# Moving the lag table, the output stage's loads and the stores inside the front of an encoder layer

## The chip, the cores and the metric

The kernel runs on one core of a Trainium2 chip. The metric is the device time of one execution in microseconds (us); lower is better. The profile names the engines PE (TensorE matmul), PEld (its weight load), DVE (VectorE), ACT (ScalarE), POOL (GpSimd) and SP (SyncE). Each engine works through its own instructions in order; SP's and POOL's also issue DMAs.

## The reference, cut to what matters

```python
h = layer_norm(x, ln_in_g, ln_in_b)                       # x: 1024 rows of 1024
proj = jnp.einsum('bld,de->ble', h, w_in)                 # 2048 columns
rq, rk, rv, rg, su, aq, ak, av = jnp.split(proj, ...)
y_ret = retention(rq, rk, rv, rg, ret_theta)              # 4 heads, chunks of 128, states forward and backward
y_ssm = s5_mixer(su, ...)                                 # 16 groups of 16 channels, 64 complex states, both ways
y_att = window_sink_attention(aq, ak, av, attn_sink)      # 8 query heads, 2 key heads, window 128
mix = concat(y_ret, y_ssm, y_att) @ w_out
h = layer_norm(ALPHA * h + mix, ln1_g, ln1_b)
ffn = expert_choice_ffn(h, router_w, w_gate, w_up, w_down)   # 16 experts, each takes its best 128 rows
h = layer_norm(ALPHA * h + ffn, ln2_g, ln2_b)

def s5_mixer(u, ...):
    lam_bar = exp(lam * step);  bu = b_bar @ u            # per group, forward and reversed
    states = associative_scan(a, b -> a2*a1, a2*b1 + b2)  # complex, along the 1024 rows
    y = gelu(real(c @ states) + d * u)
    return y * sigmoid(y @ w_glu + b_glu)
```

## The kernel before

The program has three parts. The *front* makes the input norm, all projections, the retention head group and the S5 mixer. The *attention part* makes the windowed attention, the output projection, the second norm and the router. The *expert part* streams 384 MB of expert weights and ends with the last norm. Float32 products of the projections are made of three matmuls on halves (`split` into high and low, `mm3`, lines 74 to 76).

The order inside the front is written out by hand. `front` puts functions at places on a line of numbers (`at(place, fn)`, `spread`), `Plan.run` calls them sorted by place, and every engine keeps that order. So a place sets the order on each engine and in each DMA queue; it is no time. A function that is placed early but waits holds up all that is behind it on its engines. After the front a scheduler merges the attention part's instructions with the end of the front, without changing the front's own order.

The S5 mixer works in blocks of 8 rows, so the scan runs over 128 positions. `Params` makes the powers of the decay; `outputs` and `outputs_store` make the output weights `wo_d`, which go to DRAM; `jumps` makes the powers over 8 to 128 rows (`LT`, `A`). `s5_input` stores the projected input in `ut_d`, `s5_input_load` reads it back turned as `U`, and `u_d` keeps it. `s5_states_part` multiplies it into `VS`, which holds 2 x 16 x 128 values on each partition. `s5_scan` runs 15 steps inside 8 blocks of 16 positions, then 7 steps from block to block; `s5_carry` adds the carry; `s5_states_store` writes the states `s_d`. `Lags` makes the products inside a block (the table `KC`, stored as `m_d`), and `Output` sums `m_d` times the input and `wo_d` times the states, with gelu and gate, into `YO` and `y_d`. `Matrix` loads and splits the output projection's weights.

Memory sets much of the order. Pools are opened and closed inside the front: `VS` lies where `Params` lay, so it can only be written when all of that pool has been stored. The pool `raw` has two buffers named `wraw` of 8 KB per partition, through which all weights pass. `K.ast` has three buffers under the tag `k4` (the split keys, values and queries `kst`) and three under `q2`.

The projections after the first are units named in `order`: `K0`, `K1`, `V0`, `V1` and `q00` to `q31` are products of 24 matmuls with 512 columns, `g0` to `g7` are retention gates, `r0` to `r7` retention chunks, and `l` a gap. `V0` in the code is also the place of the first unit.

## Time and profile before

| | |
|---|---|
| median of 3 runs | 1772.43 us (1767.63 to 1777.95) |
| profiled execution | 1771.64 us |
| its span from first to last instruction | 1769.9 us |
| busy: PE, DVE, ACT | 92%, 80%, 64% of the span |
| mean granted clock of PE | 0.962 |

The front ends about 392 us after the span's start, the attention part about 640 us, and the rest belongs to the experts. In the profile's lines "L643" is line 643 of the kernel, `out<-in` are the program's names, and a wait is idle time of an engine with what ended it. PEclk is the clock that was granted to PE, as a share of full speed.

### The profile page before, as it was taken

To read this page: it belongs to the slowest core of one execution; us is meant where nothing else is said; L and a number is where in the kernel's file an instruction comes from. 1 tells how busy PE (TensorE), PEld (TensorE's weight loads), DVE (VectorE), ACT (ScalarE), POOL (GpSimd) and SP (SyncE) were. 2 spreads that over 40 slices of the span, in tenths; PEclk is the share of its full clock that TensorE was granted. 3 is DMA by queue.
4 is the path that set the end of the run, shared out by engine and by line. 5 is a ranking of instruction groups with operands and counts; after the bars stand their busy time and mean duration, and the time that the engine had idled before them with its cause. 6 is when DMAs were issued, how large, how long until landed. Compare 5 with 4: busy or idle time off the path is not lost.

```text
span 1769.9 us, 21221 instructions
## 1 busy us (share of the span) xinstructions
PE 1628.6 (92%) x7760; PEld 1315.0 (74%) x7760; DVE 1415.4 (80%) x1748; ACT 1124.1 (64%) x1259; POOL 194.5 (11%) x214
## 2 busy tenths in 40 slices
PE   6987886479999989999999999999999999999996
PEld 4866775357777767888888888888888777777785
DVE  7856863154666899899888898898898989999995
ACT  4615232275555467777777777777777787777773
POOL 1000010100100101010110100100101232231221
PEclk9999988678999989999999999999999999999998
DMA  5452336853321489999999999999999999999993
GB/s 210 162 139 79 86 98 167 248 206 104 102 66 72 154 337 363 378 399 392 376 365 397 368 366 392 368 383 389 358 388 393 385 399 388 393 401 387 404 402 142
DMA packets 110713, 513.61 MB, mean 290 GB/s; under 512 B 12048, under 2 KB 35856, under 8 KB 59792
## 3 DMA queue, kind: packets, MB, share of 16 engines
q1 hardware_dynamic: 100480, 482.36, 71.9%
q0 software_dynamic: 10128, 29.89, 5.5%
q8 instruction: 61, 1.00, 0.2%
q14 instruction: 44, 0.36, 0.1%
HBM read 465.02 MB, written 47.19 MB: 289 GB/s over the span
## 4 chain that ended last, share of the span: by engine, by line
PE 58%; DVE 14%; DMA 12%; issue 8%; ACT 7%; SPq 2%; POOL 0%; POOLq 0%; DVEq 0%; ACTq 0%
PE gu L1699 24%; PE y L1699 12%; DVE whl L1746 6%; PE mm L74 4%; DMA wraw<-in_exp_w_down 4%; PE mm L75 4%; PE mm L76 4%; DMA zz<-acc_d 4%; ACT whl L1739 2%; PE tp L1684 1%; PE tp L1249 1%; ACT S L1229 1%; PE sm L1343 1%; DMA wraw<-in_exp_w_up 1%; SPq L754 1%
## 5 line engine op out<-in xcount | busy, mean ns | idle before, releaser
L1746 DVE TENSOR_TENSOR whl<-wraw,whl 128x2048 fp32r<-128x2048 f32 x384 | 873.3, 2288 | 97.9 <-ACT whl L1739 97.1
L1739 ACT ACTIVATE whl<-wraw 128x2048 fp32r<-128x2048 f32 x384 | 734.6, 1917 | 243.7 <-PE gu L1699 79.7
L1699 PE MATMUL gu<-whl,xT 128*128 128x512 f32 x3072 | 740.0, 397 | 0.0
L1699 PEld LDWEIGHTS gu<-whl,xT 128*128 128x128 f32 x3072 | 570.4, 189 | 125.1
L1699 PE MATMUL y<-whl,hT 128*128 128x512 f32 x1536 | 368.6, 395 | 0.7 <-ACT hT L65 0.7
L1699 PEld LDWEIGHTS y<-whl,hT 128*128 128x128 f32 x1536 | 288.3, 188 | 69.8 <-ACT hT L65 0.9
L1673 POOL DMA_INDIRECT xs<-h_d,index x15 | 41.3, 2756 | 741.1 <-PE y L1699 553.1
L74 PE MATMUL mm<-hT,whl 128*128 128x512 f32 x160 | 68.6, 429 | 0.5 <-ACT gate L352 0.5
L75 PE MATMUL mm<-hT,whl 128*128 128x512 f32 x160 | 65.1, 407 | 0.0
L76 PE MATMUL mm<-hT,whl 128*128 128x512 f32 x160 | 64.8, 405 | 0.0
L65 ACT ACTIVATE hT<-tp 128x512 fp32r<-128x512 f32 x80 | 45.9, 583 | 27.9 <-PE tp L1684 15.8
L66 DVE TENSOR_TENSOR hT<-tp,hT 128x512 fp32r<-128x512 f32 x80 | 54.1, 684 | 9.1 <-ACT hT L65 9.1
L74 PE MATMUL mm<-WO,yh 128*128 128x512 f32 x128 | 52.1, 407 | 4.2 <-ACT yh L65 4.0
L1684 PE MATMUL tp<-ident,hid 128*128 128x128 f32 x256 | 39.7, 279 | 14.9 <-DVE hid L1781 14.8
L1684 PEld LDWEIGHTS tp<-ident,hid 128*128 128x128 f32 x256 | 31.4, 142 | 27.0 <-DVE hid L1781 19.9
L75 PE MATMUL mm<-WO,yh 128*128 128x512 f32 x128 | 51.2, 400 | 0.0
L76 PE MATMUL mm<-WO,yl 128*128 128x512 f32 x128 | 50.4, 400 | 0.0
L1229 ACT ACTIVATE S<-S,asm 128x384 f32<-128x384 f32 (+1 forms) x64 | 36.9, 579 | 19.9 <-DVE asm L1225 19.9
L74 PE MATMUL mm<-whl,hT 128*128 128x512 f32 (+1 forms) x128 | 47.5, 371 | 1.2 <-ACT gate L352 1.2
L1222 DVE CUSTOM_DVE_ANT_0 S<-at,R,sink 128x384 f32<-128x384 f32 (+1 forms) x64 | 35.4, 579 | 15.5 <-PE at L1220 14.1
L75 PE MATMUL mm<-whl,hT 128*128 128x512 f32 (+1 forms) x128 | 45.8, 357 | 1.4 <-DVE whl L130 1.4
L76 PE MATMUL mm<-whl,hT 128*128 128x512 f32 (+1 forms) x128 | 45.3, 354 | 0.0
(426 smaller groups left out, 1837.0 us busy)
## 6 DMA issues: line engine op xcount, KB each, us to landing
wraw<-in_exp_w_gate SPq DMA_DIRECT2D x128, 1024.0 KB, 8.0
wraw<-in_exp_w_up SPq DMA_DIRECT2D x128, 1024.0 KB, 8.0
wraw<-in_exp_w_down SPq DMA_DIRECT2D x128, 1024.0 KB, 8.0
wraw<-in_w_in SPq DMA_DIRECT2D x8, 1024.0 KB, 6.0
x<-in_x SPq DMA_DIRECT2D x8, 512.0 KB, 4.5
h_d<-x SPq DMA_DIRECT2D x8, 512.0 KB, 3.1
q_d<-kst SPq DMA_DIRECT2D x32, 128.0 KB, 3.1
qs<-q_d POOLq DMA_DIRECT2D x16, 256.0 KB, 4.2
```

Of the source, the lines that this page charges most:

```text
L65: nc.scalar.activation(hi, src, AF.Copy)
L66: eng.tensor_tensor(lo, src, hi.bitcast(F32), OP.subtract)
L74: nc.tensor.matmul(ps, a[0], b[0], start=start, stop=False)
L75: nc.tensor.matmul(ps, a[0], b[1], start=False, stop=False)
L76: nc.tensor.matmul(ps, a[1], b[0], start=False, stop=stop)
L1222: nc.vector.tensor_tensor_reduce(s[:, :W], ps[:, :W], K.R[:, ro:ro + W], 2.0 ** -(h + 1), K.sink[:, h:h + 1], OP.add, OP.max, accum_out=m[ ...
L1229: nc.scalar.activation(S[g][:, :W], S[g][:, :W], AF.Exp, bias=nm[:, g:g + 1], accum_out=rs[:, g:g + 1])
L1673: nc.gpsimd.indirect_dma_start(out=xs, out_offset=None, in_=K.h1_dram, in_offset=bass.IndirectOffsetOnAxis(ap=K.index[:, e:e + 1], axis=0))
L1684: K.nc.tensor.transpose(pt[:, c, :], src[:, (c0 + c) * P:(c0 + c + 1) * P], K.ident)
L1699: nc.tensor.matmul(ps, a[s][c], u[:, t, i * w:(i + 1) * w], start=first and id(ps) not in began, stop=last and left[id(ps)] == 0)
L1739: self.K.nc.scalar.activation(u[:, 0, :], self.raw[k1].rearrange("p a b -> p (a b)"), AF.Copy)
L1746: self.K.nc.vector.tensor_tensor(u[:, 1, :], raw, u[:, 0, :].bitcast(F32), OP.subtract)
```

## The change

The change writes the front in another order and changes some instructions.

- The input norm's gain and shift are no longer broadcast by two DMAs of 512 KB. `Rows` loads two rows of 4 KB, and four matmuls with a selecting matrix spread them; ACT copies the products.
- The retention's constants, tables and states are placed earlier; half of the state steps go between the first projections.
- `outputs` and its stores stand ahead of the jumps, and the second pair of stores stands ahead of the store of `U` in SP's queue. `work` has two buffers and a third one, `wtmp`, holds the second product.
- `VS` is laid out by step: position in the block, then channel and block. A scan step reads and writes contiguous runs. The carry works on 8 channels at once (8 pairs of 840 elements for 16 pairs of 420). All states go to DRAM through ACT copies `SO` of 1024 elements.
- `Lags` is made in quarters right after the states' products, while the scan starts. It takes its buffers from `k4`, `q2` and `wraw`.
- `Output` loads its table, input and weights (`MUW`) into `wraw` buffers during the last projections. Its products are units `o0` to `o3` of the order. Weights come in rows of 128 elements out of 144.
- The turns of the retention chunks, their queries and scores, and the loads of `W6`, `W7` and the output projection's weights have other places.

```diff
-    for i in range(1, NT - 1):
-        for a in range(2):
+    for a in range(2):
+        for i in range(1, NT - 1):
...
-    return ops
+    return ops[0:NT - 2], ops[NT - 2:]
...
-        t = [self.pool.tile(sh, F32, name="work", bufs=3) for _ in range(2)]
+        t = [self.pool.tile(sh, F32, name=n, bufs=b) for n, b in (("work", 2), ("wtmp", 1))]
...
-        prev, cur = V5[:, :, :, :, r - 1], V5[:, :, :, :, r]
+        prev, cur = K.VS[:, :, r - 1], K.VS[:, :, r]
...
+def s5_states_store(K, d, ri):
...
+    SO = K.ast.tile([P, 8, P], F32, name="SO", tag="k4", bufs=3)
+    src = K.VS[:, ri, :, d * 8:d * 8 + 8, :].rearrange("p r q b -> p q b r")
+    dst = SO if d == 0 else SO[:, :, ::-1]
+    nc.scalar.activation(dst.rearrange("p q (b r) -> p q b r", r=16), src, AF.Copy)
+    for g2 in range(2):
+        nc.sync.dma_start(K.s_dram[d][g2][ri * 64:(ri + 1) * 64], SO[g2 * 64:(g2 + 1) * 64])
...
-    def load(self, g2, d):
+    def load(self, g2, d, q):
+        w = K.ast.tile([P, 4, 9, 16], F32, name="WO", tag="k4", bufs=3)
...
+        bx = K.ast.tile([P, 4, 16], F32, name="BX", tag="q2", bufs=3)
...
-            self.kc = self.pool.tile([16, 8, 15, 16], F32, name="KC")
+            self.kc = K.raw.tile([P, 8, 15, 16], F32, name="KC", tag="wraw")[0:16]
...
     def load(self, g2, q):
...
+        x = K.raw.tile([P, 4, 4, P], F32, name="MUW", tag="wraw")
+        nc.sync.dma_start(x[:, 0], K.m_dram[g2][:, gs])
+        nc.sync.dma_start(x[:, 1], K.u_dram[:, q * 8 + g2:q * 8 + 8:2, :])
+        for d in range(2):
+            n0 = 16 * (1 - d)
+            nc.sync.dma_start(x[:, 2 + d], K.wo_dram[d][g2][:, gs, n0:n0 + P])
...
+    def states(self, g2, q):
...
+            nc.sync.dma_start(z[:, :, 1 - d:P + 1 - d], K.s_dram[d][g2][:, q * 4:q * 4 + 4])
...
+class Rows:
...
+        self.x = pool.tile([P, D], F32, name="x", bufs=3)
+        for i, k in enumerate(("ln_in_g", "ln_in_b")):
+            K.nc.sync.dma_start(self.x[i:i + 1, :], I[k].rearrange("(a d) -> a d", a=1))
...
+    def select(self):
+        self.K.nc.vector.tensor_copy(self.sel, self.K.ident[0:2, 0:2, None].to_broadcast([2, 2, P]))
...
+    def spread(self, i, n):
+        K, ns = self.K, slice(n * 512, (n + 1) * 512)
+        ps = (K.pmm if i == 0 else K.pat).tile([P, 512], F32, name="mm" if i == 0 else "at")
+        K.nc.tensor.matmul(ps, self.sel[:, i, :], self.x[0:2, ns], start=True, stop=True)
+        K.nc.scalar.activation((K.g0, K.b0)[i][:, ns], ps, AF.Copy)
...
-    e = spread(B + 16.5, 0.15, par.jumps())
+    E0 = B + 26.0
+    e = B + 18.5
...
-    at(E0 + 1.0, lambda: s5_input_load(K))
-    at(E0 + 2.0, lambda: nc.sync.dma_start(K.u_dram, K.U))
+    at(E0 + 4.7, lambda: s5_input_load(K))
+    at(E0 + 5.2, WA.load)
+    at(E0 + 9.1, WG.load)
+    at(E0 + 14.0, lambda: nc.sync.dma_start(K.u_dram, K.U))
...
+    lp = [V0 - 4.0 + 1.6 * i + (1.0 if i > 3 else 0) for i in range(8)]
...
-    order = "K0 g0 g1 K1 r0 V0 r1 g2 g3 V1 r2 q00 r3 g4 g5 q01 r4 q10 r5 g6 g7 r6 q11 r7 q20 q21 l q30 l q31".split()
+    order = "K0 g0 g1 K1 r0 V0 r1 g2 g3 V1 r2 q00 r3 g4 g5 q10 r4 q01 r5 g6 g7 r6 q11 r7 q20 q30 q21 o0 o1 q31 o2 o3".split()
...
-            at(s + 8, c.turn)
+            at(s + 11, c.turn)
...
-    for k, (wt, prev) in enumerate(((W6, ("K1", "V1")), (W7, ("q01", "q11")))):
-        at(where[prev[0]] - 8, wt.load)
+    for wt, place, prev in ((W6, V0 + 15, ("K1", "V1")), (W7, where["r5"], ("q01", "q11"))):
+        at(place, wt.load)
...
+        at(max(e2 + 5.0, O + 0.2) + 0.1 * i if i < 2 else where[f"o{i - 2}"] + 3.1, lambda k=k: out.states(*k))
...
-        at(M0 + 0.1 if i < 2 else M0 + 4.6 + (i - 2) * 2.6, lambda i=i: X["mat"].load(2 * i))
+        at(where[f"o{i + 2}"] + 3.1 if i < 2 else G + 3.5 + (i - 1) * 2.5, lambda i=i: X["mat"].load(2 * i))
```

**Three places where the order changes.** First, SP's queue between the input projection of S5 and the keys. `ut_d` is the store of the projected input, `U` its turned load, `u_d` the store of that, and `wo_d` the output weights' stores. Before:

```order
L628 DMA ut_d<-uT 128x1024
L636 DMA U<-ut_d 16x16x128 x8
L1026 DMA u_d<-U 128x2048
L616 DMA wo_d_86<-work 64x1152
L616 DMA wo_d_87<-work 64x1152
L616 DMA wo_d_88<-work 64x1152
L616 DMA wo_d_89<-work 64x1152
```

The same stretch of SP's queue after:

```order
L633 DMA ut_d<-uT 128x1024
L621 DMA wo_d_86<-work 64x1152
L621 DMA wo_d_87<-work 64x1152
L641 DMA U<-ut_d 16x16x128 x8
L621 DMA wo_d_88<-work 64x1152
L621 DMA wo_d_89<-work 64x1152
L121 DMA wraw<-in_w_in 128x2048
```

The store of `U`, which waits until `U` has landed, stood ahead of three of the four pairs of output weights, and now stands behind all of them.

Second, SP's queue at the end of the projections, where the output stage's operands are loaded. `m_d` is the lag table, `q_d` the queries' store, `Z` the states. Before:

```order
L870 DMA q_d_1_76<-kst 256x1x128 x4
L754 DMA m_d_95<-KC 128x1x128 x8
L778 DMA M<-m_d_94 128x512
L780 DMA U<-u_d 128x4x128
L783 DMA WO_2862<-wo_d_86 128x576
L786 DMA Z_2864<-s_d_90 128x4x128
```

The place where `Z` is loaded after:

```order
L420 DMA y_d_71<-roT 128x256
L872 DMA q_d_1_76<-kst 256x1x128 x8
L420 DMA y_d_72<-roT 128x256
L764 DMA wg<-in_ssm_w_glu 128x512
L766 DMA bg<-in_ssm_b_glu 128x2
L790 DMA Z_2815<-s_d_90 128x4x128
L790 DMA Z_2818<-s_d_92 128x4x128
L790 DMA Z_2821<-s_d_90 128x4x128
L790 DMA Z_2824<-s_d_92 128x4x128
```

The lag table's stores are gone from here, the table, the input and the weights are loaded further ahead, and only the states still wait here, behind eight stores of queries.

Third, ACT at the end of the front. `KC` is the lag table, `kst` the last queries, `WO` with four digits the split of the output projection's weights, `YG` the gelu, `yT` its turned copy, `glu` the gate, and L1229 (after: L1255) the attention's exponentials. Before:

```order
L742 ACTIVATE KC<-at 16x4x128 x2
L744 ACTIVATE KC<-at 16x4x112 x2
L68 ACTIVATE kst<-mm,qscale 128x512
L65 ACTIVATE WO_2912<-wraw 128x1024 x2
L803 ACT_TABLE_LOAD
L803 ACTIVATE YG<-mm 128x4x8x16
```

ACT at the same end after:

```order
L68 ACTIVATE kst<-mm,qscale 128x512
L805 ACTIVATE YG<-mm 128x4x8x16 x2
L814 ACTIVATE yT<-tp 128x512 x4
L65 ACTIVATE WO_2992<-wraw 128x1024 x2
L827 ACTIVATE glu<-mm,hb 128x512
L1255 ACT_TABLE_LOAD
L1255 ACTIVATE S,asm<-S,asm 128x256
```

The lag table has left this place, and the four gelus stand together ahead of the weights' split, where they stood between its parts.

More of the change, by code (lines that the diff above doesn't have):

```diff
@@ L606, in outputs @@
         cr, ci = (self.C[:, i, q, None, :].to_broadcast(sh) for i in range(2))
-        t = [self.pool.tile(sh, F32, name="work", bufs=3) for _ in range(2)]
+        t = [self.pool.tile(sh, F32, name=n, bufs=b) for n, b in (("work", 2), ("wtmp", 1))]
         ve.tensor_tensor(t[0], cr, pr if ri == 0 else ni, OP.mult)
@@ L923, in front @@
     par = Params(K, I, X["s5a"])
-    norm[2].load()
-    spread(3.5, 0.01, ops[0:10])
+    at(6.0, norm[2].load)
+    at(2.9, rows.select)
+    for i in range(2):
+        for n in range(2):
+            at(3.3, lambda i=i, n=n: rows.spread(i, n))
+    spread(3.5, 0.01, ops[0:6])
     at(4.0, norm[0].stats)
-    spread(4.5, 0.01, ops[10:])
-    at(5.0, decays)
     at(7.0, norm[0].gain)
@@ L981, in front @@
         at(place, fn)
+    ahead, behind = retention_state(K)
+    for i, fn in enumerate(ahead):
+        at(S0 + T * (i + 3) + 2.55, fn)
     B = S0 + T * NT
@@ L1052, in front @@
     SC = E0 + 23.8
[L1053 to L1054 removed]
+    e = spread(SC, 3.7, steps)
+    e = spread(e, 1.6, blocks)
     fixes = s5_carry(K)
[L1056 to L1062 removed]
+    e2 = spread(e, 3.8, fixes)
+    for i in range(4):
+        at(e + (i + 1) * 7.6 + 0.05, lambda i=i: s5_states_store(K, i // 2, i % 2))
+    at(e2 + 1.0, lambda: close(X["s5v"][0]))
+    lag = lambda: X["lags"]
+    quarters = [(g2, d, q) for g2 in range(2) for d in (1, 0) for q in range(2)]
+    lp = [V0 - 4.0 + 1.6 * i + (1.0 if i > 3 else 0) for i in range(8)]
+    for i, (k, s) in enumerate(zip(quarters, lp)):
+        at(E0 + 18.0 + i * 0.1 if i < 3 else lp[i - 3] + 0.5, lambda k=k: lag().load(*k))
+        at(s, lambda k=k: lag().part(*k))
+        at(s + 1.0, lambda k=k: lag().put(*k))
+        if k[1:] == (0, 1):
+            at(s + 1.4, lambda k=k: lag().store(k[0]))
     ops, exps = retention_tables(K)
[L1066 to L1068 removed]
+    spread(E0 + 2, 0.3, ops)
+    at(E0 + 8.5, exps)
+    spread(E0 + 9.5, 1.0, behind)
     at(V0 - 0.9, lambda: X.update(retB=pool("retB", side="right")))
@@ L1075, in front @@
     where = {}
+    X["out"] = Output(K, I)
+    out = X["out"]
+    qs = [(g2, q) for g2 in range(2) for q in range(2)]
     for w in order:
@@ L1125, in front @@
             at(where[prev[i]] + 6.0, lambda wt=wt, i=i: wt.low(i))
-    R = where["r7"] + 12.5
-    def lags_space():
-        close(X["retB"][0], K.c_ret)
-        X["s5k"] = pool("s5k", side="right")
-        X["lags"] = Lags(K, I, X["s5k"][1])
-    at(R, lags_space)
-    lag = lambda: X["lags"]
-    quarters = [(g2, d, q) for g2 in range(2) for d in (1, 0) for q in range(2)]
-    at(R + 0.1, lambda: (lag().load(0, 1), lag().load(0, 0)))
-    lp = [R + 5 + 1.5 * i for i in range(8)]
-    for i, (k, s) in enumerate(zip(quarters, lp)):
-        at(s, lambda k=k: lag().part(*k))
-        at(s + 1.0, lambda k=k: lag().put(*k))
-        if i in (1, 3):
-            at(s + 1.1, lambda d=k[1]: lag().load(1, d))
-        if k[1:] == (0, 1):
-            at(s + 1.2, lambda k=k: lag().store(k[0]))
@@ L1144, in front @@
-    Z = R + 5 + 8 * 1.5 + 1.3
+    R = where["r7"] + 2.9 + 12.5
+    at(R, lambda: close(X["retB"][0], K.c_ret))
+    O = max(R, e2 + 1.0) + 0.1
     def output_space():
         X["s5o"] = pool("s5o")
-        X["out"] = Output(K, I, X["s5o"][1])
-    at(max(R + 3, e2 + 2.1), output_space)
-    out = lambda: X["out"]
-    qs = [(g2, q) for g2 in range(2) for q in range(2)]
-    end = where["q31"] + 5.6
-    O0 = max(Z + 5, end - 2.0)
+        out.space(X["s5o"][1])
+        out.bias()
+    at(O, output_space)
@@ L1154, in front @@
     for i, k in enumerate(qs):
[L1155 to L1158 removed]
+        at(where["q11"] + 8.5 + i * 0.1 if i < 2 else where[f"o{i - 2}"] + 3.0, lambda k=k: out.load(*k))
+        at(max(e2 + 5.0, O + 0.2) + 0.1 * i if i < 2 else where[f"o{i - 2}"] + 3.1, lambda k=k: out.states(*k))
@@ L1159, in front @@
+    G = s + 1.0
     mq = [(m, q) for q in range(2) for m in range(2)]
     for i, k in enumerate(mq):
-        at(G + i * 0.6, lambda k=k: out().turn(*k))
-        at(G + 2.6 + i * 2.0, lambda k=k: out().gate(*k))
-        at(G + 4.6 + i * 2.0, lambda k=k: out().gated(*k))
-    at(G + 12.0, lambda: (out().store(0), out().store(1)))
+        at(G + i * 0.6, lambda k=k: out.turn(*k))
+        at(G + 2.6 + i * 2.0, lambda k=k: out.gate(*k))
+        at(G + 4.6 + i * 2.0, lambda k=k: out.gated(*k))
```

188 lines of the change are left out of this document (81 added, 107 removed).

## Prediction

> **What bounds the kernel now.** PE carries most of the work, so what can be won lies where it waits. After the page I cut the span where the program changes its work and asked for each engine's busy time in each stretch (the view of windows):
>
> ```profile
> 121.00:157.60 36.60, 20.69 (x107) 18.47 (x108) 9.32 (x24) 12.45 (x20) 0.74 (x8) 0.81 0.46 101
> 157.60:281.90 124.30, 110.60 (x654) 94.80 (x653) 98.41 (x271) 46.75 (x105) 9.71 (x9) 0.93 0.36 99
> 281.90:321.60 39.70, 24.75 (x113) 17.16 (x112) 3.23 (x10) 6.67 (x13) 1.33 (x6) 0.79 0.58 153
> 321.60:392.20 70.60, 40.80 (x172) 30.90 (x173) 25.80 (x63) 35.08 (x67) 6.92 (x15) 0.71 0.78 252
> 392.20:650.00 257.80, 236.50 (x1205) 187.10 (x1203) 180.77 (x498) 147.00 (x306) 22.43 (x66) 0.95 0.37 131
> ```
>
> The columns are PE, PEld, DVE, ACT and POOL busy, then PE's granted clock. The front ends at 392.2 with the last `YO`. Inside it three stretches are poor: 121.0 to 157.6, and above all 281.9 to 392.2, where nobody is busy even half of the time but PE, and PE runs at a clock of 0.7 to 0.8. The attention part (PE busy 92% of its time), and the experts behind it, start on what the front delivers, so time won in the front moves all behind it. The view of waits, for PE alone, names the gaps; its numbers are total, times, longest:
>
> ```profile
> PE at L643 <- ACT VS L648: 8.6, 1, 8.6
> PE at L643 <- DMA U<-ut_d: 7.5, 1, 7.5
> ...
> PE tp L415 <- DVE ro L409: 7.7, 3, 3.8
> PE po L383 <- DVE sT L377: 4.3, 1, 4.3
> PE mm L74 <- ACT gate L352: 1.7, 2, 1.2
> ...
> PE mm L795 <- DMA U<-u_d: 9.7, 2, 8.0
> PE at L732 <- ACT KC L742: 8.9, 1, 8.9
> ```
>
> The first two lie in 121.0 to 157.6, the next three in 157.6 to 281.9, the last two behind. The reader sees a chain of DRAM round trips: lag table out, lag table in, products.
>
> **Part 1, the head (0 to 121): +1 us.** The two broadcasts go; four matmuls and four ACT copies come.
>
> ```profile
> rsmall<-in_ret_theta SPq DMA_DIRECT2D x1, 4.0 KB, 3.0
> ...
> 10.60 1.27 DVE L155 SCALAR_TENSOR_TENSOR x<-x,l0mv,gb 128x1024 f32<-128x1024 f32 x1
> ...
> 381.05 5.42 PE mm L817 x8
> ```
>
> DVE reaches the gain (L155) at 10.60 behind the retention's small operations; 18 of these move behind tile 1, so the gain could start about 2 us sooner. But the shift needs four float32 matmuls of 512 columns: the rows of 4 KB, issued near 1.7 by my estimate, land 3.0 later like `rsmall`, at 4.7, and L817 (8 rows for 4 such matmuls) took 5.4 us, so the last copy is ready near 11. The shift gains 1 us, and the 18 operations then stand in DVE's queue ahead of tile 1's `hT`: I count 0 (bounds -3 and +3). The six state steps on DVE lie beside PE's projections. With two `work` buffers the third `inputs` call waits from its first operation instead of its second, one operation about as long as L155: +1.
>
> **Part 2, 121.0 to 157.6: -6 us.** The wait for `U` stays: the store of `ut_d`, eight loads behind it.
>
> ```profile
> 102.40 0.19 DVE L525 COPY LT<-PA 128x32 f32<-128x32 f32 x1
> ...
> 106.46 1.35 DVE L608 TENSOR_TENSOR work<-C,PA 128x1152 f32<-128x1152 f32 x1
> ...
> 110.50 1.09 SPq L616 DMA_DIRECT2D wo_d<-work  x2
> 128.61 10.00 SPq L616 DMA_DIRECT2D wo_d<-work  x6
> ...
> 136.14 1.36 DVE L610 TENSOR_TENSOR work<-work 128x1152 f32<-128x1152 f32 x1
> 141.67 2.41 ACT L648 ACTIVATE VS<-at 64x512 f32<-64x512 f32 x4 [20.22 <-DMA wo_d<-work]
> ...
> wo_d<-work SPq DMA_DIRECT2D x8, 288.0 KB, 4.3
> WO<-wo_d SPq DMA_DIRECT2D x4, 576.0 KB, 4.8
> wraw<-in_w_in SPq DMA_DIRECT2D x8, 1024.0 KB, 6.0
> ```
>
> SP stored `u_d`, which waits for `U`, before it could store six of the eight `wo_d` (128.61); DVE's last product waited for their buffer and ended at 137.5; the last store landed at 141.6, and only then could ACT write `VS` into that memory. In the new queue the stores stand ahead of `u_d`, and without the jumps ahead of them (102.40 to 106.46) DVE's last product should end near 124: from 102.4, 12 operations of 1.36, then by my estimate 3 us of the retention's tables and 2 us of waiting for the first store. Issue 1.1 and landing 4.3 give 129.5; behind it in the DMAs are `U` and 1 MB of weights (6.0), so I take 133 for the first `VS`, 8.7 us sooner. Bounds: 129.5, as if alone, and 141.7, as before. Three lag quarters now come in here, 8 rows of 0.98 us each time (below): +2.9. Sum -5.8.
>
> **Part 3, 157.6 to 281.9 (K0 to q20): -10 us.** The waits of L415, L383 and L74 are 13.7 us. The turn of a chunk moves 3 places back, so it finds `ro` ready; state steps, tables and exponentials leave this stretch, so `sT` is in time. After such a wait PE runs at half clock for some 4 us:
>
> ```profile
> 185.00:190.00 5.00, 5.00 (x15) 3.71 (x14) 4.93 (x11) 0.00 (x0) 0.00 (x0) 0.50 0.58 129
> 293.44 0.98 PE at L732 x8
> L663 DVE TENSOR_TENSOR sc<-VS,A x15: 566/584/627, 156.6 to 222.8; 128x256 f32<-128x256 f32 x15
> L665 DVE TENSOR_TENSOR sc<-sc,sc x15: 424/425/427, 157.8 to 224.0; 128x256 f32<-128x256 f32 x15
> L648 ACT ACTIVATE VS<-at x16: 588/592/594, 141.7 to 156.0; 64x512 f32<-64x512 f32 x16
> L624 ACT ACTIVATE uT<-mm x4: 592/596/601, 88.6 to 109.9; 128x512 f32<-128x512 f32 x4
> ```
>
> That is about 2 us each, three times: -6. Against it five lag quarters (4.9 us), which were in the next stretch; a wait of the last of them, since its load stands behind eight stores of the table on SP (5.7 us in the row of L754 below): +2.4; and `W6` and `W7`, whose loads now stand so late that ACT reaches their split before they land (6.0 us): +2 on PE, the rest hidden under units that need no ACT. Sum -10.4. Bounds: -22 if none of these waits comes, +5 if they replace the old ones.
>
> The scan's operations on strided runs (L663, 584 ns) become contiguous like L665 (425 ns), some 0.5 us a step, 7 us in all on DVE; cover, since PE sets the pace. `VS` is now written by ACT in steps of 512 bytes. Row L624 already writes scattered and takes 596 ns, like the contiguous L648 at 592: I charge nothing. The Trainium skill's page "SBUF — State Buffer" (Door 1: The DMA port swizzle) says that accesses within one 16-byte line run at full rate and that each step to a new line costs. Sixteen copies of 512 elements would then each pay twice what L663 pays for 256, 0.32 us, 5 us of ACT ahead of the first unit, and the sum would be some 3 us less. The trace shows that price on DVE and not on ACT.
>
> **Part 4, 281.9 to 392.2: -52 us.** It was 110.3 us. In the new order it holds q30, q21, q31 and four products, then the tail.
>
> ```profile
> 301.62 5.74 SPq L754 DMA_DIRECT2D m_d<-KC  x8
> 277.69 2.64 SPq L870 DMA_DIRECT2D q_d<-kst  x4
> 148.33 1.95 PE L643 MATMUL at<-U,win 128*128 128x128 f32 x16
> 277.41 0.39 PE L74 MATMUL mm<-hT,whl 128*128 128x512 f32 x1
> 278.10 0.39 PE L74 MATMUL mm<-hT,whl 128*128 128x512 f32 x1
> ...
> wraw<-in_w_out SPq DMA_DIRECT2D x4, 1024.0 KB, 7.1
> WO<-wo_d SPq DMA_DIRECT2D x8, 288.0 KB, 8.4
> Z<-s_d SPq DMA_DIRECT2D x8, 256.0 KB, 7.8
> ...
> 347.76 2.00 ACT L65 ACTIVATE WO<-wraw 128x1024 fp32r<-128x1024 f32 x2 [25.48 <-DMA wraw<-in_w_out]
> 348.84 2.36 DVE L66 TENSOR_TENSOR WO<-wraw,WO 128x1024 fp32r<-128x1024 f32 x2 [16.21 <-ACT WO L65]
> ```
>
> Three units are 72 matmuls at 0.23 us (0.69 between every third): 16.6. The products are 96 rows of 0.11 (1.95 for 16, overlapped): 11. New waits: the states' loads stand behind q30's store, so from q30's end 1.4 (split) + 2.6 (four issues) + 2.8 (six loads, somewhat quicker) + 4.8 (landing, the row of 576 KB on a quiet queue) = 11.6, while PE has q21 for 5.6: 6 us. The third and fourth products' operands can only be loaded into `wraw` when the first and second are done: 8.4 landing and some 2 of issue against o1 and q31 (8.3): 2, then 1. With the half clock behind them, 2, waits make 11. The tail, from the last product to the last `YO`: the third load of `w_out` needs the first to land (7.1) and to be split (3.4, from 347.76 to 351.20), lands 7.1 later and is split 3.4 later, and the gates stand around these splits in ACT's queue; less the lead of the first load (one product, 2.7) and with two last gates (about 2): 20. Sum 16.6 + 11 + 11 + 20 = 58.6, so -51.7. Bounds: -70 with no waits and the gates ahead of the third split, -30 if operands land as late as they did (U 8.0, Z 7.8) each time.
>
> A rule bears on these waits. PE ran at 0.50 in 185 to 190 after 4.3 us of waiting. By "TensorE: Matmul & The Clock Gate" (What's actually happening) of the Trainium skill, half rate follows an idle window of about 3.4 us; by that the waits of 2 and 1 us cost no clock, and the sum would gain 1 us.
>
> **The sum.** The profiled execution took 1771.6 us, 1.7 more than its span and 0.8 under the median of 1772.4. +1 - 6 - 10 - 52 = -67, behind 392.2 nothing: 1705. The attention part may pay back a few us, since it filled gaps of the old tail: 15 of its score operations on DVE lie before the last `YO` in either order, so I count nothing (bounds -3 and +10).
>
> **Rivals.**
> - *The projections don't get shorter.* The late `W6` and `W7`, the lag waits and the states' loads take what the old waits cost: part 3 at +5, part 4 at -38, sum -38, 1734. For it: ACT and DVE stand still behind a split that waits, and both carry chunk work. Against: PE has units there that need no ACT.
> - *The waits don't come.* Part 3 at -20, part 4 at -62: sum -87, 1685. For it: SP may run ahead of its places. Against: `Z` stands behind q30's store by order.
> - *SP becomes the bound, and it gets slower.* Between K0 and the first product SP must issue about 108 DMAs in order (lag loads, 16 table stores, keys, queries, chunks, operands). At 0.6 us (5.74 for 8) that is 65 us beside 140. It decides when one issue costs 1.9 us or more in the mean, over 200 us: 60 us more than planned and the whole gain gone, 1790. Against: the rows here are at 0.55 to 0.72 us.
> - *The front isn't what the attention part waits for.* Then a shorter front changes nothing, 1770. Against: PE's first attention products wait for `KHL`, its split for `w_out`, and 392 to 650 is 92% PE.
>
> **How the numbers follow.** Forecast (1691 to 1719) 0.50; waits don't come 0.22; projections no shorter 0.20; attention not waiting 0.04; SP bound 0.04. What can be told from no change is about 0.5%, 9 us. Faster 0.92 (the first three), same 0.04, slower 0.04. The likeliest case gives 1705. The range takes in both neighbours with their bounds: 1680 to 1738.
>
> **What would show it.** The first `VS` copy near 133 instead of 141.7; no wait of L415 for `ro`; lag rows between the units; first `YO` to last `YO` near 325 instead of 392; the stretch behind it as long as before. I'd be wrong if `VS` still waits for `wo_d`, if ACT's waits for `W6` and `W7` reach PE in full, or if the part behind the last `YO` grows by as much as the front shrank.

## The result, and the profile after

| | before | after |
|---|---|---|
| median | 1774.4 us (4 runs) | 1727.6 us (4 runs, 1726.2 to 1729.7) |
| profiled span | 1769.9 us | 1726.2 us |
| end of the last `YO` | 394.6 us | 348.2 us |
| first product of the output projection with the low half `yl` | 417.8 us | 372.5 us |

The ratio after to before is 0.974, with a 95% interval of 0.971 to 0.977: 47 us less, inside the range that was given (1680 to 1738), and 23 us above the single figure (1705). In the profiled spans it is 43.7 us: the last `YO` comes 46.4 us sooner, and behind it 2.7 are paid back (1375.3 us to the span's end before, 1378.0 after).

The view of windows of the changed kernel, cut where its own stages end: the first key product starts at 156.24, the product q20 ends at 270.6, q30 and q21 end at 282.1, the last output product and its transposes at 313.3, the last `YO` at 348.2. The columns are those of the rows in the prediction.

```profile
121.00:156.24 35.24, 29.20 (x154) 23.15 (x152) 19.77 (x64) 23.01 (x26) 0.75 (x8) 0.90 0.66 189
156.24:270.60 114.36, 107.54 (x663) 92.77 (x663) 77.68 (x233) 50.88 (x104) 11.26 (x9) 0.94 0.49 126
270.60:282.10 11.50, 11.50 (x53) 9.37 (x51) 1.83 (x3) 2.59 (x8) 0.00 (x0) 1.00 1.03 297
282.10:313.30 31.20, 19.32 (x123) 17.68 (x122) 3.47 (x7) 4.57 (x7) 7.20 (x23) 0.84 0.85 229
313.30:348.20 34.90, 23.96 (x79) 13.99 (x78) 21.99 (x62) 26.84 (x63) 2.17 (x4) 0.76 0.74 244
348.20:606.00 257.80, 237.11 (x1222) 187.09 (x1221) 186.72 (x500) 148.65 (x305) 21.50 (x59) 0.97 0.39 140
```

The rows of before in the prediction are cut at other places than it says. K0 starts at 158.8 there, not at 157.6. At 281.9 it is q21 that ends; q20 ends at 276.0, as ACT's copies of both products (`kst`) show. And 392.2 is the end of the third of four `YO`; the last one starts at 393.45. These rows, and the windows of before cut at the same stages as those above:

```profile
276.96 0.70 ACT L68 ACTIVATE kst<-mm,qscale 128x512 fp32r<-128x512 f32 x1
281.96 0.69 ACT L68 ACTIVATE kst<-mm,qscale 128x512 fp32r<-128x512 f32 x1 [1.00 <-PE mm L76]
...
393.45 1.16 DVE L827 TENSOR_TENSOR YO<-glu,yT 128x512 f32<-128x512 f32 x1
```

```profile
158.80:276.00 117.20, 103.50 (x623) 89.35 (x622) 93.13 (x262) 43.52 (x99) 8.94 (x8) 0.93 0.35 98
276.00:394.60 118.60, 73.70 (x325) 54.25 (x323) 35.57 (x89) 45.50 (x87) 9.35 (x22) 0.76 0.70 211
```

From K0 to q20 PE is busy 107.5 of 114.4 us, where it was 103.5 of 117.2. The stretch from q20's end to the last `YO`, 118.6 us before, takes 77.6. Two poor stretches are left in it: 31.2 us with 19.3 of PE, and the tail of 34.9 us with the clock at 0.76. The view of waits of the changed kernel, for PE, names what stands in them:

```profile
PE mm L801 <- DMA Z<-s_d: 10.7, 1, 10.7
PE mm L819 <- ACT glu L827: 5.2, 1, 5.2
...
PE at L728 <- DMA BX<-bx_d: 3.5, 1, 3.5
...
PE at L648 <- DMA wo_d<-work: 3.3, 1, 3.3
PE po L383 <- DVE sT L377: 3.0, 1, 3.0
```

The waits for `KC`, for `U` in the output stage and for `ro` are gone. One long wait, for the states `Z`, is left, and a new one for the gate's `glu`.

### The profile page after: what moved, and what is told of

It is laid out like the page before. It is cut to its first block, busy times and chain, and to the rows that moved or that the text cites. A ratio compares the mean times of both kernels' runs of the same rounds, so it can differ in the third digit from the quotient of the medians.

```text
span 1726.2 us, 21249 instructions
## 1 busy us (share of the span) xinstructions
PE 1623.0 (94%) x7768; PEld 1305.1 (76%) x7768; DVE 1406.8 (81%) x1733; ACT 1133.3 (66%) x1259; POOL 196.5 (11%) x214
## 4 chain that ended last, share of the span: by engine, by line
PE 51%; DMA 10%; DVE 10%; issue 7%; ACT 4%; SPq 1%; POOL 0%; POOLq 0%; DVEq 0%; ACTq 0%
PE gu L1725 26%; PE y L1725 13%; DVE whl L1772 5%; DMA zz<-acc_d 3%; DMA wraw<-in_exp_w_down 3%; ACT whl L1765 2%; PE mm L74 2%; PE mm L76 2%; PE mm L75 2%; DMA wraw<-in_exp_w_gate 2%; PE tp L1710 2%; DMA wraw<-in_exp_w_up 1%; PE tp L1275 1%; DMA wraw<-in_w_out 1%; SPq L872 1%
## 5 line engine op out<-in xcount | busy, mean ns | idle before, releaser
L74 PE MATMUL mm<-hT,whl 128*128 128x512 f32 x160 | 66.8, 417 | 0.0
L74 PE MATMUL mm<-WO,yh 128*128 128x512 f32 x128 | 52.4, 410 | 1.5 <-ACT yh L65 1.4
L1255 ACT ACTIVATE S<-S,asm 128x384 f32<-128x384 f32 (+1 forms) x64 | 36.9, 579 | 17.2 <-DVE asm L1251 17.1
L74 PE MATMUL mm<-whl,hT 128*128 128x512 f32 (+1 forms) x128 | 47.3, 369 | 0.5 <-ACT hT L65 0.5
L1807 DVE TENSOR_TENSOR hid<-hid,gu 128x512 f32<-128x512 f32 x64 | 43.5, 679 | 1.9 <-PE gu L1725 1.9
L76 PE MATMUL mm<-whl,hT 128*128 128x512 f32 (+1 forms) x128 | 44.3, 346 | 0.0
```

The source lines that it names most:

```text
L74: nc.tensor.matmul(ps, a[0], b[0], start=start, stop=False)
L76: nc.tensor.matmul(ps, a[1], b[0], start=False, stop=stop)
L1255: nc.scalar.activation(S[g][:, :W], S[g][:, :W], AF.Exp, bias=nm[:, g:g + 1], accum_out=rs[:, g:g + 1])
L1807: at(self.after, q, 3, lambda: nc.vector.tensor_tensor(self.h[q], self.h[q], self.pg[q][1], OP.mult))
```

## The experiments

Every kernel below is the changed kernel with one edit, unless said otherwise. The kernel before was timed beside each group of them (medians from 1769.8 to 1774.4 us), so that runs of different groups are better compared by the ratio than by the median. The intervals of the ratios are about 0.0035 wide to each side, 6 us, so one edit of a few us can seldom be told by its time; the two runs with all edits together differ clearly from the changed kernel in their times, and the run with the stores' order undone nearly does. The place of each effect is read from the profile, and that is one execution: half clock of PE comes in some executions and not in others behind the same wait (shown under "The rule on the clock"), so a shift of 1 to 2 us between two profiles need not be the edit.

| run | median, us | ratio to before, interval | last `YO` ends | PE's wait for `Z`, total |
|---|---|---|---|---|
| changed kernel | 1727.6 | 0.9741 (0.9709 to 0.9774) | 348.2 | 10.7 |
| e9_ud, stores' order undone | 1737.3 | 0.9809 (0.9770 to 0.9848) | 359.9 | 11.7 |
| e4_turn, turns undone | 1729.6 | 0.9754 (0.9724 to 0.9784) | 347.4 | 4.7 |
| e10_late, operands late | 1726.0 | 0.9753 (0.9718 to 0.9788) | 353.4 | 12.0 for `MUW` |
| e1_runs, `VS` in runs | 1724.2 | 0.9732 (0.9694 to 0.9770) | 343.0 | 11.1 |
| e8_w7, `W7` earlier | 1720.1 | 0.9716 (0.9678 to 0.9754) | 341.8 | 12.6 |
| e2_states, states earlier | 1728.6 | 0.9731 (0.9687 to 0.9775) | 351.9 | 6.7 |
| e5_turn7, last chunk earlier | 1721.7 | 0.9731 (0.9694 to 0.9768) | 344.3 | 9.5 |
| e3_wout, four buffers | 1727.7 | 0.9750 (0.9720 to 0.9779) | 337.5 | 10.5 |
| e6_wout2, two buffers | 1717.6 | 0.9698 (0.9662 to 0.9735) | 342.4 | 17.6 |
| e7_head, small operations later | 1728.0 | 0.9758 (0.9720 to 0.9797) | 350.9 | 12.4, put down to `q_d` |
| e11_all, four edits | 1705.1 | 0.9637 (0.9603 to 0.9672) | 325.9 | 12.9 |
| e12_all2, and splits early | 1699.6 | 0.9612 (0.9576 to 0.9647) | 323.3 | 13.8 |

**The order of SP's stores, undone.**

```diff
-    at(E0 + 4.7, lambda: s5_input_load(K))
+    at(E0 + 0.1, lambda: s5_input_load(K))
-    at(E0 + 14.0, lambda: nc.sync.dma_start(K.u_dram, K.U))
+    at(E0 + 0.2, lambda: nc.sync.dma_start(K.u_dram, K.U))
```

> Only the order of SP's queue goes back: the loads of U and the store of U stand ahead of the last three pairs of output weights' stores. Theory: these stores then wait for U, DVE's fourth product waits for their buffer, and the first copy into VS starts near 141 again (133.2 in the changed kernel); the end is 7 us later (5 to 9). Rival: without the jumps in between DVE and the stores are early enough; VS within 2 us, the time within 2 us.

The timeline of DVE and of SP in this run, and its row for the copies into `VS`:

```profile
134.99 1.36 DVE L613 TENSOR_TENSOR work<-C,NI 128x1152 f32<-128x1152 f32 x1 [13.81 <-DMA wo_d<-work]
...
128.52 0.34 SPq L1056 DMA_DIRECT2D u_d<-U  x1
128.91 4.99 SPq L621 DMA_DIRECT2D wo_d<-work  x4
...
L654 ACT ACTIVATE VS<-at x16: 1021/1056/1090, 144.1 to 163.0; 64x512 f32<-64x512 f32 x16
```

The old picture is back, row for row: SP waits for `U` until 128.5, DVE stands 13.8 us before its fourth product, and `VS` starts at 144.1. The last `YO` is 11.7 us later and the time 10 to 12 (by the medians and by the ratios), more than the 7 expected: `VS` starts 2.4 us later than in the kernel before (141.7), since with two buffers of `work` the fourth product waits from its first operation, and its copies are the slow ones of the run on `VS` below. The reason given for part 2 is shown.

**The turns, undone.**

```diff
-            at(s + 11, c.turn)
-            at(s + 11.5, c.store)
+            at(s + 8, c.turn)
+            at(s + 8.5, c.store)
```

> The turns and stores of the retention chunks go back to 8 places behind the chunk's start, from 11. Theory: the three waits of PE for ro (7.7 us before, none after) come back with half clock behind them: +8 us (5 to 14), with PE's L415 waiting for ro again. Rival: ro was late before because of the tables, exponentials and state steps that left this stretch; without them no wait comes back and the time stays within 3 us.

The view of waits of this run, PE between 200 and 282, and from 282 on:

```profile
PE tp L415 <- DVE ro L409: 7.7, 4, 4.2
...
PE mm L801 <- DMA Z<-s_d: 4.7, 2, 3.3
```

The mechanism came back to the tenth (7.7 us), but not the time: the last `YO` is not later (347.4 for 348.2), since the wait for `Z` shrank from 10.7 to 4.7. PE arrived later at a place where it would have stood anyway. So a part of the gain in the projections was not cashed in the changed kernel: it was waited away at `Z`.

**The operands of the first output products, late.** The states are kept apart from the other operands, so that these can be loaded behind them.

```diff
-        at(where["q11"] + 8.5 + i * 0.1 if i < 2 else where[f"o{i - 2}"] + 3.0, lambda k=k: out.load(*k))
+        at(where["o0"] - 0.3 + i * 0.1 if i < 2 else where[f"o{i - 2}"] + 3.0, lambda k=k: out.load(*k))
```

> The table, the input and the weights of the first two output products are loaded behind the last projections and behind the states' loads, no longer during the projections. Theory: the first product then waits for them, some 4 us longer than for Z (293 becomes 297), and the time is 4 us longer (2 to 6): this is what the early loads bring as things stand, since Z waits at the same place. Rival 1: they land within the wait for Z, 0. Rival 2: the loads are worth the whole round trip, 10 us or more.

PE now waits 12.0 us for `MUW` and the first product starts at 296.4 instead of 293.0, 3.4 us later, the last `YO` 5.2 later. The time did not show it (ratio 0.9753 beside 0.9741). As the changed kernel stands, loading these operands early is worth 3 to 5 us at its place and no more, because `Z` is late at the same place.

**`VS` written in runs.**

```diff
-        dst = K.VS[...].rearrange("p r q b -> p q b r")
+        dst = K.VS[...].rearrange("p r q b -> p q r b")
-        K.nc.scalar.activation(dst, src.rearrange("p q (b r) -> p q b r", r=16), AF.Copy)
+        K.nc.scalar.activation(dst, src.rearrange("p q (b r) -> p q r b", r=16), AF.Copy)
```

> The copies into VS run in the order chunk, step, block instead of chunk, block, step: ACT writes runs of 32 bytes and reads the product with a stride, the stored values are the same. Theory: the scattered writing makes a copy of 512 values take 1.06 us in the changed kernel where it took 0.59 before; then the 16 copies fall to about 0.59 each, the last ends about 7 us sooner (151.9 to about 145), and the kernel gains 5 us (2 to 7) on 1727.6. Rival 1: reading with a stride costs ACT as much as writing with one; the copies stay near 1.06 and the time stays. Rival 2: the copies shorten but PE has other work there; gain under 2 us.

The rows of the copies (shortest, median and longest ns, first and last start), of the changed kernel and of this run:

```profile
L654 ACT ACTIVATE VS<-at x16: 1022/1058/1108, 133.2 to 150.8; 64x512 f32<-64x512 f32 x16
```

```profile
L654 ACT ACTIVATE VS<-at x16: 588/592/597, 132.1 to 145.3; 64x512 f32<-64x512 f32 x16
```

Same values, same number of elements, and 592 ns for 1058. The last `YO` ends 5.2 us sooner. The strided reading that this puts in its place costs nothing. So the scattered writing of ACT had a price, 16 x 0.466 = 7.5 us of ACT. Only part of it lay on the path: when PE comes to its wait for the lag rows' `BX` (169.6 in the changed kernel, 165.0 here) this run is 4.6 us ahead, and 1.1 of these it had before its first copy, so the copies account for some 3.5. The Trainium skill's page "SBUF — State Buffer" (Door 1: The DMA port swizzle) has it: every step of an access to another 16-byte line costs. The run agrees, with its 512-byte steps at 1058 ns and its 32-byte runs at 592.

**`W7` one store earlier in SP's queue.**

```diff
-    for wt, place, prev in (..., (W7, where["r5"], ("q01", "q11"))):
+    for wt, place, prev in (..., (W7, where["r3"], ("q01", "q11"))):
```

> The load of the last projection weights W7 stands ahead of a store of queries in SP's queue, before chunk r3, instead of at r5. Theory: ACT's wait of 6.0 us for it (241.5 to 247.5) held up the chunks' work, with PE's wait for sT (3.0 us) and half clock until 260 behind it; without it q20 ends 4 us sooner and the kernel gains 3 to 4 us. Rival: the buffer of W7 is not free earlier, or the wait is under other work: 0.

Two rows of the changed kernel, ACT's split of `W7` and the chunk product of PE behind it, the windows of the changed kernel from 250 to 262, then two of them in this run:

```profile
247.50 1.06 ACT L125 ACTIVATE whl<-wraw 128x1024 fp32r<-128x1024 f32 x1 [6.03 <-DMA wraw<-in_w_in]
...
250.20 0.69 PE L383 MATMUL po<-kv,sT 128*128 128x64 f32 x2 [3.05 <-DVE sT L377]
...
250.00:254.00 4.00, 3.80 (x18) 3.68 (x20) 3.93 (x14) 1.57 (x2) 0.33 (x1) 0.50 0.00 0
254.00:258.00 4.00, 4.00 (x15) 3.20 (x16) 2.60 (x6) 2.67 (x8) 1.31 (x1) 0.50 0.57 138
258.00:262.00 4.00, 4.00 (x16) 3.12 (x16) 3.93 (x14) 1.94 (x1) 0.18 (x1) 0.76 0.09 28
```

```profile
250.00:254.00 4.00, 4.00 (x21) 3.24 (x20) 3.83 (x13) 1.72 (x3) 0.00 (x0) 1.00 0.23 68
254.00:258.00 4.00, 4.00 (x27) 3.62 (x26) 3.90 (x7) 2.62 (x7) 1.63 (x1) 1.00 0.55 131
```

Both waits and the half clock are gone; the first output product comes at 285.7 instead of 293.0 and the last `YO` 6.4 us sooner, nearly twice what was expected. Behind its wait of 3.05 us PE had worked at half clock for 9.7 us (250.2 to 259.9, by windows of 1 us), which cost it 4.9 us more. In eight other profiles with this wait (2.8 to 3.4 us) the half clock lasts 6.8 us, so this gain varies by more than 1 us from one execution to the next.

**The states, earlier.** The first run moves the last chunk's turn and the place `R` behind which its memory is free, the second only the turn.

```diff
-            at(s + 11, c.turn)
-            at(s + 11.5, c.store)
+            dt = 3.0 if w == "r7" else 0.0
+            at(s + 11 - dt, c.turn)
+            at(s + 11.5 - dt, c.store)
...
-    R = where["r7"] + 2.9 + 12.5
+    R = where["r7"] + 2.9 + 9.5
```

> Only the last retention chunk is turned and stored 3 places earlier, and the places that wait for its memory move with it: its store, the gate's weights and the loads of the states then stand in SP's queue ahead of eight stores of queries instead of behind all of them. Theory: PE's wait for Z (10.7 us) is the queue and the memory of the last chunk; it falls to about 3 us, the last YO comes 8 us sooner (348.2 to about 340) and the kernel gains 8 us (6 to 10). Rival 1: the states land no sooner, since the DMAs are busy there; 0 to -2. Rival 2: PE now waits for ro of the last chunk, 3 us, and half of the gain goes.

> Only the last retention chunk is turned and stored 3 places earlier; the places of the gate's weights and the states' loads stay behind the queries' stores. Theory: in the run that moved all of it, the queries' stores came to stand behind the loads and PE got a new wait for kst (6.4 us); with the queue as it is, only the store's landing falls out of the chain, the wait for Z goes from 10.7 to about 5, as in the run with all turns moved (4.7), and the kernel gains 5 us (3 to 7). Rival: what is won ahead of the products is lost behind them, because the attention's scores and not YO set the end: 0 to -2.

SP's timeline of the changed kernel ahead of `Z`, PE's waits in the first run, and SP's timeline of the second run from the store of the last chunk on:

```profile
265.66 2.67 SPq L872 DMA_DIRECT2D q_d<-kst  x4
...
275.65 6.38 SPq L872 DMA_DIRECT2D q_d<-kst  x8
282.13 0.55 SPq L420 DMA_DIRECT2D y_d<-roT  x1
...
285.36 2.08 SPq L790 DMA_DIRECT2D Z<-s_d  x4
```

```profile
PE mm L801 <- DMA Z<-s_d: 6.7, 4, 4.5
PE mm L799 <- DVE kst L69: 6.4, 1, 6.4
```

```profile
281.02 0.55 SPq L420 DMA_DIRECT2D y_d<-roT  x1
281.67 2.50 SPq L872 DMA_DIRECT2D q_d<-kst  x4
...
285.35 2.08 SPq L790 DMA_DIRECT2D Z<-s_d  x4
```

PE's first product with `Z`, in the changed kernel and in the second run:

```profile
292.95 1.49 PE L801 MATMUL mm<-MUW,Z 128*128 128x128 f32 x4 [10.73 <-DMA Z<-s_d]
```

```profile
289.27 0.77 PE L801 MATMUL mm<-MUW,Z 128*128 128x128 f32 x2 [7.49 <-DMA Z<-s_d]
292.03 0.77 PE L801 MATMUL mm<-MUW,Z 128*128 128x128 f32 x2 [1.99 <-DMA Z<-s_d]
```

Neither theory held. `Z` is issued no sooner: at 285.35 in the second run, 285.36 in the changed kernel, and 285.25 in the first run. In the first run PE's wait for `Z` is shorter only because PE first waits 6.4 us for `kst`: the queries' stores behind the loads free its buffer late, a new wait in place of the old one, and the last `YO` is 3.7 us later. In the second run the first `Z` is used 3.9 us after its issue, where it was 7.6 in the changed kernel; PE then waits 2.0 us more for the next one, the last product ends 2.0 us sooner and the last `YO` 3.9. The run with all turns moved shows the same: `Z` was issued at 288.4 and used at 291.9. Its wait of 4.7 us had been read wrongly, since PE came to this place 6.3 us later there. Why `Z` lands sooner behind its issue in these two runs is open.

The rows of the changed kernel show a queue without a pause: from 265.66 to 282.68 SP issues 24 DMAs, 17.0 us or 0.7 each, while the DMAs are full (1.03 in the window from 270.6), then the last chunk's store lands and `Z` follows. The first run took four DMAs out of this queue: from its first store of queries to the issue of `Z` it is 18.2 us where it was 19.7, but the queue began 1.4 us later. Whether the count, the full DMAs or the landing holds `Z` most stays open; another queue for `Z` was not tried.

**The loads of `w_out`.** Four buffers of their own behind the last projection, or two, issued at the first output product.

```diff
-        self.raw[c] = self.K.raw.tile([P, 2, 1024], F32, name="wraw")
+        pl = self.pool if c < 2 * 4 else self.K.raw          # second run: 2 * 2
+        self.raw[c] = pl.tile([P, 2, 1024], F32, name="wor" if c < 2 * 4 else "wraw")
...
+        X["wor"] = pool("wor", bufs=4)                       # second run: bufs=2, at where["o0"] + 0.2
+        X["mat"].pool = X["wor"][1]
-        at(where[f"o{i + 2}"] + 3.1 if i < 2 else G + 3.5 + (i - 1) * 2.5, lambda i=i: X["mat"].load(2 * i))
+        at(where["q31"] + 5.71 + 0.01 * i if i < 4 else where[f"o{i + 2 - 4}"] + 3.1, lambda i=i: X["mat"].load(2 * i))
+        # second run: at(where["o0"] + 0.3 + 0.01 * i if i < 2 else where[f"o{i}"] + 3.1, ...)
```

> The four loads of w_out get four buffers of their own and are issued right behind the last projection, where they waited for the operands' two buffers. Theory: the tail of 35 us from the last product to the last YO is the chain of two buffers (load, split, load, split); without it the last YO comes some 15 us sooner (348.2 to about 333) and the kernel gains 15 us. Rival 1: the DMAs are the limit, since 3 MB of keys and values for the attention start at the same time; 7 MB at the 380 GB/s of that stretch take until 325, the first w_out lands no sooner than 317, and the gain is 8 us or less. Rival 2: the rest does not wait for YO; the last YO moves and the time stays.

> Two of the four loads of w_out get buffers of their own and are issued when the first output product starts, into DMAs that are 0.6 busy; the other two take the operands' buffers as before. The attention's tables do not wait for this memory, which they did in the run with four buffers (first scores held up until 342). Theory: the tail is the loads of w_out, which land 13 us after issue beside 3 MB of keys and values and wait for two buffers; without that the last YO comes 12 us sooner (348.2 to 336) and the kernel gains 10 us. Rival: YO is not what the rest waits for; the last YO moves by as much, the first output product (369.9) and the time by less than 3 us.

The DMA stretch of the changed kernel (the window from 300 to 324), its row of the loads' issue, and its DMA rows from 300 to 350 for the loads that share it (KB each, median us to landing; of the four loads of `w_out` only the first two have their landing on record, 13.0 and 13.1):

```profile
300.00:324.00 24.00, 18.89 (x112) 14.93 (x111) 3.98 (x11) 5.50 (x9) 5.58 (x10) 1.00 1.14 346
...
310.14 27.84 SPq L884 DMA_DIRECT2D wraw<-in_w_out  x4
...
wraw<-in_w_out SPq DMA_DIRECT2D x4, 1024.0 KB, 13.0
KHL<-k_d POOLq DMA_DIRECT2D x4, 512.0 KB, 7.5
AV<-v_d POOLq DMA_DIRECT2D x2, 512.0 KB, 15.2
```

Four buffers, POOL's table for the attention and PE's wait:

```profile
339.71 0.46 POOL L1225 IOTA S<- 128x384 f32 x1 [29.84 <-DVE WO L66]
...
342.91 0.58 PE L1249 MATMUL at<-KHL,qs 128*128 128x256 f32 x1 [10.80 <-DVE asm L1252]
```

With four buffers the last `YO` came 10.7 us sooner and the time not at all. The attention's tables lie where the new buffers lay, so the scores that had filled the tail began only when the last split was done. It was not YO alone that the rest waited for: scores and `YO` have to be there both. With two buffers these tables do not wait; the last `YO` is 5.8 us sooner, the first `yl` product 4.2. In the profiled run the span is 10 us shorter, of which 5 lie in the experts, whose stretch varies by such amounts between kernels; the time's interval holds 4 us as well as 10. The gain was half of what the theory said, since the earlier loads took the DMAs from the other two products: the waits for `Z` grew from 10.7 to 17.6.

**The head.**

```diff
-    spread(S0 + 1.4, 0.01, ops[6:])
-    at(S0 + 2.7, decays)
+    spread(S0 + 5.8, 0.005, ops[6:])
+    at(S0 + 5.95, decays)
```

> The 18 small operations of the retention's constants stand behind the split of tile 1 on DVE, where they stood ahead of it. Theory: they cost the head the wait of 4.0 us at the second turn (24.6) and some of the 2.7 us by which the later tiles are late; the tiles' turns come 2 to 3 us sooner and so does the end: -2.5 us. Rival: later waits of the front (the output weights' store at 128) take it up again: 0.

The wait at the second turn stayed (3.9 us, now for `x` of L158), and PE got a wait of 2.8 us for `ktok`, which needs the moved constants. The turn of the last tile came at 75.4, against 74.3 in the changed kernel and 71.6 before. The theory fell; what the head's 2.8 us come from was not settled.

**All together.** `VS` in runs, the last chunk's turn, `W7`, and two buffers for `w_out`, whose loads now are issued during q30; then also the first two splits behind the last projection.

```diff
+    at(e2 + 1.05, matrix_raw)
+        at(where["q30"] + 1.0 + 0.01 * i if i < 2 else where[f"o{i}"] + 3.1, lambda i=i: X["mat"].load(2 * i))
...
-        at(G + 3.4 + i * 2.5, lambda i=i: X["mat"].parts(2 * i))
+        at(where["q31"] + 5.8 + i * 0.1 if i < 2 else G + 3.4 + i * 2.5, lambda i=i: X["mat"].parts(2 * i))
```

> Four edits together: VS written in runs of 32 bytes, the last chunk turned 3 places earlier, W7 loaded ahead of a store of queries, and two loads of w_out into buffers of their own, now issued during the projection q30. Theory: each removes a wait at a place of its own, so that they add up: 4 + 3 + 6 + 7 = 20 us less than 1727.6, 1708 (1702 to 1715), ratio to the kernel before 0.964. Rival: the attention's scores set the end, and behind 12 us nothing more is to be had: 1715 or more.

> As the run before it, and the first half of the output projection's weights is split right behind the last projection, during the last two products, where ACT and DVE idle. Theory: the gates then stand behind two splits fewer, and the last YO comes 4 us sooner than without: 1704 (1698 to 1712). Rival: the split delays the gelu of the third product on ACT by 4 us and the same time is lost there: no difference to the run before it.

The rows of the last step and the loads of the first of these runs, then the splits on ACT of the second:

```profile
L829 DVE TENSOR_TENSOR YO<-glu,yT x4: 1086/1105/1111, 313.8 to 324.8; 128x512 f32<-128x512 f32 x4
DMA to landing us min/median/max: 5.3/6.4/7.5
```

```profile
297.26 3.88 ACT L65 ACTIVATE WO<-wor 128x1024 fp32r<-128x1024 f32 x4
```

The edits add up: 1705.1 us against the 1708 expected (a ratio of 0.964, as expected), and with the splits 1699.6, the last `YO` 2.6 us sooner where 4 were expected, a ratio of 0.961 to the kernel before (0.958 to 0.965), clear of the changed kernel's 0.974. Moved away from the keys and values, the loads of `w_out` land in 6.4 us for 13.0. The wait for `Z` is still there (12.9 and 13.8 us).

## Why the prediction was right or wrong, point by point

The sign and the range were right, and the waits that were to go went; the size was not right: -67 was forecast, about -44 came in the profiled spans. By its own parts, cut where the stages end:

| part | forecast | measured |
|---|---|---|
| head and 121 to K0 | +1 - 5.8 = -4.8 | 158.8 to 156.2: -2.6 |
| K0 to q20 | -10.4 | 117.2 to 114.4: -2.8 |
| q20's end to the last `YO` | 58.6 in place of 118.6: -60.0 (its own sum: 110.3 to 58.6, -51.7) | 118.6 to 77.6: -41.0 |
| behind the last `YO` | 0 | +2.7 |

The prediction cut the old stretches wrongly. Its 124.3 us for K0 to q20 held q21 as well (5.9 us), and the 58.6 us of the new last stretch hold q21 once more; and its 392.2 falls short of the last `YO` by 2.4 us. Its own terms therefore give -75 and not -67. The terms are 31 us off and the single figure only 23; that the figure is the nearer of the two is luck.

Of the 47 us, the runs that undo one step bring back 10 to 12 (the order of the stores), 3 to 5 at their place (the late operands) and nothing in the time (the turns). No run put the lag table back behind the projections. That its leaving made the largest part, the 41 us at the end of the front, is read from the two profiles alone: PE's waits for `KC` (8.9) and for `U` (9.7) and the lag rows are gone from there.

**Part 2: the first copy right, its price wrong.** The first `VS` copy was put at 133 and came at 133.2, by the cause given. The step that failed is the sentence that charged nothing for the scattered writing. Row L624, on which it rested, was misread: that copy reads with a stride and writes in long runs. The rule of the Trainium skill was told, with its price of 5 us of ACT and 3 us of the sum, and put aside on that row; the copies cost 7.5 us more of ACT and some 3.5 us on the path.

**Part 1.** The forecast was +1, and the last tile's turn is 2.8 us later, within the bounds of -3 and +3. The cause is open.

**Part 3: the waits nearly right, the half clock wrong.** No wait of L415 or L74 is left and the lag rows stand between the units. 13.7 us of waiting became 6.8 (3.5 for the lag load, where 2.4 was taken, 3.0 for `sT` behind the late `W7`, where 2 was taken, and 0.3), which is -6.9 for the forecast's -9.3. The step that failed is the half clock: the forecast took 6 us off for the three old waits and charged nothing behind the two new ones. By windows of 1 us PE works at half clock in 183.5 to 190.4, 223.1 to 227.9 and 251.8 to 255.2 before, 15.1 us, and in 174.6 to 178.0 and 250.2 to 259.9 after, 13.1 us. At a clock of 0.50 half of that time is lost, so 1.0 us was won here and not 6. With the five lag quarters (4.9) these terms give the measured -2.8 within 0.2 us.

**Part 4: two terms mis-sized.** First, the wait of the first product, 6 us in the forecast and 10.7 in the trace. The sum began with q30's end and counted ten issues from there; SP was then still in the middle of a queue of 24. From q30's end (276.3) it was 9.1 us to the issue of `Z` (6.8 in the forecast) and 7.6 from there to the product (4.8). The first of the two is the rival of an SP that sets the pace, not over the whole stretch (where it would have decided at 1.9 us an issue) but in one place and at 0.7; what lengthened the second is open. From q20's end to the last product it took 42.7 us in all instead of 38.6.

Second, the tail: 20 us in the forecast, 34.9 in the trace. Rows of ACT, the first and the third split of `w_out`, and of DVE, the end of the third split and the last `YO`; then the window in which the third load of `w_out`, issued at 327.44, moves (the last column is GB/s):

```profile
323.15 2.00 ACT L65 ACTIVATE WO<-wraw 128x1024 fp32r<-128x1024 f32 x2 [6.69 <-DMA wraw<-in_w_out]
...
336.16 1.99 ACT L65 ACTIVATE WO<-wraw 128x1024 fp32r<-128x1024 f32 x2
...
343.36 1.22 DVE L66 TENSOR_TENSOR WO<-wraw,WO 128x1024 fp32r<-128x1024 f32 x1
...
347.12 1.10 DVE L829 TENSOR_TENSOR YO<-glu,yT 128x512 f32<-128x512 f32 x1
```

```profile
328.40:331.40 3.00, 2.81 (x8) 1.60 (x6) 1.38 (x4) 3.00 (x10) 0.00 (x0) 0.50 0.97 325
```

From the last product's end to the first split it is 9.9 us (7.1 less a lead of 2.7, 4.4, in the forecast), from there to the third split 13.0 (3.4 + 7.1 = 10.5), and from there to the end of the last `YO` 12.0 (3.4 + 2 = 5.4). The first is the landing: 7.1 us was taken from a row of before, but here 3 MB of keys and values were issued on POOL's queue from 306.5 to 310.8, the DMAs were full (1.14 from 300 to 324), and the first two loads took 13.0 and 13.1. The second is not the landing: the third load could be issued 4.3 us after the first split began, and 325 GB/s over 3 us are its 1 MB, so it had moved by 331.4; its split began at 336.16 without a wait of ACT. In between ACT worked on the second split, a gate and the attention's exponentials. The third is DVE: the attention's scores stand between the splits there, the third split ended 8 us after ACT began it, and two `YO` were queued behind it. The forecast had counted the attention's work at nothing; the landing explains 5.5 of the 14.6 us, the queues of ACT and DVE the other 9.1. That fits the run with two buffers, where earlier loads brought half of what had been expected of them.

**The rivals.** The measured time is nearest to the one of "the projections don't get shorter" (1734), and that mechanism came in part: K0 to q20 got 2.8 us shorter instead of 10.4, since the lag wait and the late `W7`, with the half clock behind them, took most of it back (the rival had +5). The larger part of what was missing lay in the tail. That the front is not what the rest waits for is refuted with one limit: in all runs but one the last `YO` and the end move together (1372 to 1381 us between them), and in the run with four buffers, where the scores were late, they did not (1388).

**The rule on the clock.** The row weighed was 4.3 us; this trace adds one with 3.05 us of waiting (250.20, above) and a clock of 0.50 from 250 to 258. By the Trainium skill's "TensorE: Matmul & The Clock Gate" (What's actually happening) an idle window of about 3.4 us is wanted for that. Here somewhat less was enough. For the waits of about 2 us, which the forecast had charged with half clock, the traces go both ways: PE waits 1.9 us for `work` (L597, near 99) in all 13 profiles of the new order (with four transposes behind it, 2.3 us lie between two products), and the half clock comes behind this wait in seven of them and not in the other six. The same window behind it, in the changed kernel and in the run with the states earlier (the column before the last two is the clock):

```profile
101.50:104.80 3.30, 3.30 (x18) 2.75 (x17) 3.27 (x4) 1.59 (x3) 0.00 (x0) 1.00 0.40 159
```

```profile
101.50:104.80 3.30, 3.30 (x10) 2.46 (x9) 3.27 (x4) 0.95 (x2) 0.00 (x0) 0.50 0.40 159
```

So the length of the wait alone does not decide. Nor does it set how long the half clock lasts: 6.8 us around the wait of 4.3 in the kernel before (183.5 to 190.4; the forecast had taken some 4, and its own row from 185 to 190 is longer than that), 3.4 behind one of 3.8 there (251.8 to 255.2), 10.2 around the one of 3.05 here (249.7 to 259.9). All stretches of half clock ahead of the last `YO` in these two profiles last one to five times 3.4 us.
